# Gates and gated unit merged into the mixers' schedule, and the group norm's squares summed before the column sums, in a hybrid encoder layer on one Trainium2 core

## The chip, the core and the metric

The kernel runs on one core of a Trainium2 chip. A core has five engines with an instruction queue each: TensorE (PE: matmuls, with PEld its weight loads), VectorE (DVE), ScalarE (ACT), GpSimd (POOL) and SyncE (SP), which issues most of the DMAs. The on-chip memory is SBUF; matmuls write to PSUM. The metric is the time of one launch on the device in microseconds (us), as a median of several executions.

## The reference

One layer of a streaming encoder over 1024 tokens of width 1024, float32. The parts that the change touches:

```python
y = rms_norm(x)                        # norm 1
y @ w_in  ->  xa, gate (512 each: recurrence), u (512: state space)
# RG-LRU group
xc = causal_conv4(xa) + conv_b
r, i = sigmoid(xc @ wa + ba), sigmoid(xc @ wx + bx)      # by heads
a = exp(-8 * r * softplus(-lam))
h_t = a_t * h_{t-1} + sqrt(1 - a_t^2) * (i_t * xc_t)
A = h * gelu(gate)
# S5 group: diagonal complex state space in 32 groups of 16 channels
B = gelu(ssm(u) + d_skip * u)
B = B * sigmoid(B @ glu_w + glu_b)                       # gated unit
x = x + concat[rms_norm_A(A), rms_norm_B(B)] @ w_out
x = x + peer(rms_norm(x))              # product-key experts
out = rms_norm(x)
```

`peer` scores each token against two sets of 128 keys for 8 heads, takes 16 of the 256 best pairs and adds those experts' outputs.

## The kernel before, in words

`front()` does everything up to the output projection and takes about the first 430 us; `peer()` takes the rest. Activations are held transposed: features on the 128 partitions, tokens along the free dimension, ordered so that eight strided sets s of 128 tokens lie one behind the other. An fp32 product is made of three matmuls: each factor is split into a rounded part and a rest (names with h and l: `xh`, `xl`), and h*l, l*h and h*h are summed in PSUM. ACT makes the rounded part, DVE the rest. All compute instructions are recorded through one helper, so their profile lines all say L146, and the tile names tell them apart.

The mixers of `front()`:
- `us_first` and `us_second` project the two halves of the state-space input into the tiles `Vt[0]` and `Vt[1]` (PSUM tile `usp`).
- `quarter(q)`, four times, is the state-space group: it builds small operators (`WB`, `CAr`, `kp`), transposes `Vt` (`utp`), makes the inputs (`inr`, `ini`), rotates and scans them (`Wr`, `Zr`), makes the outputs (`yp`), applies gelu and stores into `yB`.
- `proj(grp)` makes 256 columns of the other projections in the PSUM tile `pj`: groups 0 and 1 the recurrence inputs `xa[0..3]`, groups 2 and 3 the gates. A group has 96 matmuls with 512 columns; the weights are loaded and split ahead in `wr`, `wh`, `wl`.
- `lru(m)`, four times, is the recurrence of 128 channels: convolution (`xc`), two gates (`gt`, sigmoid), tanh, exp, sqrt and a scan, which leaves its result in `xa[m]`.

Then follow `gates` and `last` (gelu of each `gate`, and `yA = xa * gate`), `glu` (splits `wg` and `yB`, makes `glp` with 96 matmuls, sigmoid `sg`, product into `yB`), `norm(0)` and `norm(1)` (split `yA` into `ah`, `al` and the new `yB` into `gh`, `gl`, square into `sq`, and sum over channels in `gs`), and `w_out(0)`, `w_out(1)`: 192 matmuls `wop` each, of which twelve make one half of a token block; their result times the group's `rg` is added to `h`. In `w_out(1)` the squares of the new `h` are summed (`jk`, `ss`) for norm 2. `peer()` starts with norm 2: `g2` is loaded, `xn = h * r2 * g2` is made for the blocks 5 to 7, transposed (`x2t`), split (`xGh`, `xGl`) and multiplied with the query weights (`wqr`, split into `wqh`, `wql`; result `qp`).

The order on each engine is fixed when the program is built. The class `Merge` holds a modelled time for each engine and runs Python generators as threads: the thread with the least time plus bias goes next, until its next `yield`; a `yield` of a name waits until another thread has set that flag. `mg.run` runs a list of (bias, thread) to its end. Engines then work in the order so recorded, and semaphores keep the data dependences. Before, there are three such runs one behind the other: mixers (state space 0.0, projections 1.0, recurrences 3.0), then gates and `last`, then gated unit, norms and output projection together.

SBUF is given out in two stacks, left and right, of pools that are closed in reverse order; a tile in the place of an older one waits until that one's last reader is done. ACT also issues some DMAs, in order with its own work: the eight loads of `h` and that of `g2` among them.

Of the kernel before, what the change touches and what calls it, by code (L numbers as in the profile page):

```python
# [18 lines left out]
P = 128  # L19
# [130 lines left out]
def front(tc, a, cst, nd, mg):  # L150
# [28 lines left out]

    pset = pools.open("fset")  # L180
# [76 lines left out]
    def us_first():  # L257

        w, held = [], [(pu if s < 2 else pj if s < 4 else pt)("usp")[:, :256] for s in range(L)]
        ws = wgroup(1024, 256, w, w0)  # L260
        for k in range(8):
            split_x(k)
            next(ws)
            yield
            for s in range(L):
                us_product(held[s], s, k, w)
            yield
        mg.flag("x")
        yield "rc"
        Vt[0] = p5.tile([P, 16, L, 16], F32, name="Vt", tag="Vt", bufs=2)  # L270
        for s in reversed(range(L)):
            us_out(0, s, held[s])
            yield
        mg.flag("us0")

    def us_second():
        w = []
        yield from wgroup(1280, 256, w)
        Vt[1] = p5.tile([P, 16, L, 16], F32, name="Vt", tag="Vt", bufs=2)
# [153 lines left out]
    def quarter(q):  # L433
# [71 lines left out]
        for h in range(2):  # L505
# [5 lines left out]
            S.activation(UT[:, 4 * h:4 * h + 4], q3(pp), AF.Copy)  # L511
        pq = [pt("inr"), pt("ini")]
# [164 lines left out]
    def s5_thread():  # L677
        yield "set"
        for q in range(4):
            yield from quarter(q)  # L680

    def proj_thread():
        yield from us_second()
        for grp in range(2):
            yield from proj(grp, [x[:, 3:] for x in xa[2 * grp:2 * grp + 2]], False)

    def lru_thread(ms):
# [3 lines left out]
        mg.flag("lru")  # L691

    lr_ = lru_thread(range(4))
    mg.run([(0.0, s5_thread()), (1.0, proj_thread()), (3.0, lr_)])
    pools.close("f5", "fset")
    pya = pools.open("fya")
    yA = [pya.tile([P, T], F32, name=f"yA{m}") for m in range(4)]
    pgate = pools.open("fgate")
    gate = [pgate.tile([P, T], F32, name=f"gate{m}") for m in range(4)]
    def gates():  # L700
        for grp in range(2):
            yield from proj(2 + grp, gate[2 * grp:2 * grp + 2], True)

    def last():
        for m in range(4):
            if m % 2 == 0:
                yield f"proj{2 + m // 2}"
            S.activation(gate[m], gate[m], AF.Gelu_apprx_tanh)
            sc = lambda x: x.rearrange("p (s c) -> p s c", c=P)
            V.tensor_tensor(sc(yA[m]), xa[m][:, 3:].rearrange("p (c s) -> p s c", s=L), sc(gate[m]), ALU.mult)  # L710
            yield

    mg.run([(0.0, gates()), (0.0, last())])
    pools.close("fl", "fw", "fin", "fxa")
    pools.close("fgate")


# [3 lines left out]
    ah = pg.tile([P, 4, T], F32R, name="ah")  # L721
    al = pg.tile([P, 4, T], F32R, name="al")
    po = pools.open("fo")
# [3 lines left out]
    wo = [{}, {}]  # L727

    def glu():
        for k in range(4):  # L730
            wg = pgw.tile([P, 512], F32, name="wg", tag="wg", bufs=2)
# [7 lines left out]
        for h in range(2):  # L739
            sl = slice(512 * h, 512 * h + 512)  # L740
            for ct in range(4):
# [7 lines left out]
                sg = pgw.tile([P, 512], F32, name="sg", tag="sg", bufs=2)  # L749
# [3 lines left out]
        mg.flag("glu")  # L753

# [16 lines left out]
    def norm(grp, ys, dh, dl):  # L771

        gs = pu("gs")
        for k in range(4):
# [5 lines left out]
            sq = po.tile([P, T], F32, name="sq2", tag="sq2")  # L780
            S.activation(sq, ys[k], AF.Square)
            yield
            for s in range(L):
                PE.matmul(gs[:, 4 * s + k:4 * s + k + 1], sq[:, s * P:(s + 1) * P], ones, start=True, stop=True)
            yield
        V.tensor_reduce(rg[grp], gs[:, :4 * L].rearrange("p (s k) -> p s k", k=4), AX.X, ALU.add)
        rsqrt_cols(mg, rv, rg[grp], rg[grp], 1.0 / 512)
# [37 lines left out]
    def group_b():  # L825
        yield from glu()
        yield from norm(1, [yB[:, k] for k in range(4)], gh, gl)
        yield from w_out(1)

    mg.run([(0.0, group_b()), (0.5, norm(0, yA, ah, al)), (1.0, group_a())])  # L830
    pools.close("fgw")
    pools.close("fo", "fg", "fya", "fkeep", "fps")
# [790 lines left out]
```

## Time and profile before

| what | us |
|---|---|
| median of 3 executions | 2782.96 (2782.08 to 2785.82) |
| the profiled execution | 2788.28 |
| its span, first to last instruction | 2786.5 |
| mean granted clock of TensorE, share of full | 0.957 |

| stretch of the span | what runs |
|---|---|
| 0 to 58 | loads, squares of `x`, first half of the state-space input, set-up |
| 58 to 291 | mixers, gates, the last product into `yA` |
| 291 to 430 | gated unit, group norms, output projection |
| 430 to 441 | norm 2 of the first blocks, first query weights |
| 441 to 2786 | PEER |

Times of rows are counted from the first instruction of the profiled execution. The span is 1.8 us shorter than that execution's time, and that execution is 5.3 us above the median, so differences are read inside the span and put onto the median. A row's idle time in brackets, with the sign <-, is the time in which the engine stood before it, and what ended it. ACTq and SPq are the DMA issues of these engines. Busy shares of PE come from modelled ends, so that a busy PE may still work slower than it could; the granted clock says how fast.

### The profile page before, as it was taken

What the parts mean: (1) busy time and instruction counts of PE and PEld (TensorE: products, weight loads), DVE (VectorE), ACT (ScalarE), POOL (GpSimd) and SP (SyncE); (2) the same over time, 40 slices, a digit from 0 to 9 for tenths busy, and PEclk for the clock granted to TensorE, in tenths of its full rate; (3) what the DMA queues carried; (4) which work ended last, traced back from release to release, by engine and by line L of the source; (5) the groups of instructions that cost most, each with busy time, mean ns of one, the idle gap of its engine ahead of it and who ended that gap; (6) DMA issues with size and microseconds to landing.
All of it is one profiled execution on the core that took longest, in us unless ns stands there. A gap on an engine that the chain in (4) does not pass through costs nothing.

```text
span 2786.5 us, 40983 instructions
## 1 busy us (share of the span) xinstructions
PE 2561.9 (92%) x14719; PEld 2314.2 (83%) x14719; DVE 2359.6 (85%) x4536; ACT 1322.1 (47%) x2401; POOL 1153.7 (41%) x777
## 2 busy tenths in 40 slices
PE   5888899888899999989989889999989999999997
PEld 5765688887799899989989878888878888888885
DVE  7787435499998999989989869999888889899996
ACT  5356424222286494773955753333433444333332
POOL 0000000023375474864745634455545555445550
PEclk9898899999999999999999989999999999999998
DMA  5110315366699899998998999999989999999994
GB/s 166 26 30 25 121 61 164 121 231 191 221 342 397 291 378 364 311 382 287 392 371 273 393 338 333 328 330 324 332 303 324 332 331 331 329 332 329 326 338 137
DMA packets 302140, 761.84 MB, mean 273 GB/s; under 512 B 28784, under 2 KB 126384, under 8 KB 296816
## 3 DMA queue, kind: packets, MB, share of 16 engines
q0 software_dynamic: 110592, 402.70, 40.4%
q1 hardware_dynamic: 184464, 345.19, 35.2%
q10 hardware_dynamic: 6880, 11.33, 1.2%
q8 instruction: 116, 1.90, 0.3%
q14 instruction: 88, 0.72, 0.1%
HBM read 668.81 MB, written 89.13 MB: 272 GB/s over the span
## 4 chain that ended last, share of the span: by engine, by line
PE 58%; DVE 23%; DMA 8%; ACT 6%; issue 5%; SPq 0%; ACTq 0%; DVEq 0%
PE vp L146 23%; PE ap L146 14%; PE total L146 6%; PE qp L146 4%; DVE row L146 3%; ACT ohB L146 3%; PE wop L146 3%; DVE hb L146 3%; DMA A_d<-aa 2%; DVE ix L146 2%; DVE ul L146 2%; PE gp L146 2%; DVE oh L146 2%; DMA ur<-in_uT_dram 2%; DVE v L146 2%
## 5 line engine op out<-in xcount | busy, mean ns | idle before, releaser
L1138 POOL DMA_INDIRECT row<-in_peer_u_dram,idx x384 | 569.2, 1482 | 1047.2 <-PE qp L146 541.2
L1138 POOL DMA_INDIRECT row<-in_peer_v_dram,idx x384 | 581.8, 1515 | 484.0 <-DVE hb L146 366.7
L146 PE MATMUL ap<-xDl,uh 128*128 128x320 f32 x2048 | 656.1, 320 | 19.5 <-ACT aa L146 19.2
L146 PE MATMUL ap<-xDh,ul 128*128 128x320 f32 x2048 | 650.9, 318 | 17.1 <-DVE ul L146 16.9
L146 PE MATMUL ap<-xDh,uh 128*128 128x320 f32 x2048 | 647.3, 316 | 0.0
L146 DVE SCALAR_TENSOR_TENSOR hb<-row,act,hb 128x1024 f32<-128x1024 f32 x384 | 492.0, 1281 | 7.3 <-DMA hb<-H_d 3.1
L146 DVE CUSTOM_DVE_ANT_0 row<-row,xg 128x1024 f32<-128x1024 f32 x384 | 458.3, 1217 | 6.0 <-DMA xg<-X_d 5.0
L146 PE MATMUL vp<-vl,hh 128*128 128x512 f32 x1024 | 400.2, 391 | 13.9 <-DVE h L146 11.6
L146 PEld LDWEIGHTS ap<-xDl,uh 128*128 128x128 f32 x2048 | 392.7, 192 | 22.9 <-ACT aa L146 20.9
L146 PEld LDWEIGHTS ap<-xDh,ul 128*128 128x128 f32 x2048 | 393.0, 192 | 22.1 <-DVE ul L146 20.7
L146 PE MATMUL vp<-vh,hl 128*128 128x512 f32 x1024 | 400.0, 391 | 0.0
L146 PE MATMUL vp<-vh,hh 128*128 128x512 f32 x1024 | 400.0, 391 | 0.0
L146 PEld LDWEIGHTS ap<-xDh,uh 128*128 128x128 f32 x2048 | 392.3, 192 | 0.0
L146 ACT ACTIVATE gq<-gt 128x640 f32<-128x640 f32 x128 | 175.1, 1368 | 337.9 <-DVE hr L146 325.8
L146 PE MATMUL gp<-ohB,ohA 128*128 128x128 f32 x1280 | 211.6, 285 | 44.1 <-ACT gs L146 23.6
L146 DVE TENSOR_TENSOR ul<-ur,uh 128x1024 fp32r<-128x1024 f32 x128 | 156.1, 1220 | 108.8 <-ACT uh L146 106.4
L146 PEld LDWEIGHTS vp<-vl,hh 128*128 128x128 f32 x1024 | 193.0, 188 | 55.2 <-DVE h L146 12.9
L146 PEld LDWEIGHTS gp<-ohB,ohA 128*128 128x128 f32 x1280 | 187.9, 195 | 53.4 <-ACT gs L146 25.5
L146 PEld LDWEIGHTS vp<-vh,hh 128*128 128x128 f32 x1024 | 192.9, 188 | 40.3
L146 PEld LDWEIGHTS vp<-vh,hl 128*128 128x128 f32 x1024 | 192.9, 188 | 39.4
L146 ACT ACTIVATE aa<-ap 128x320 f32<-128x320 f32 x194 | 85.1, 439 | 261.7 <-PE ap L146 237.7
L146 ACT ACTIVATE ohB<-ohB,kt 128x128 f32<-128x128 f32 x480 | 204.5, 503 | 0.0
(422 smaller groups left out, 4548.7 us busy)
## 6 DMA issues: line engine op xcount, KB each, us to landing
ur<-in_uT_dram SPq DMA_DIRECT2D x128, 512.0 KB
vr<-in_peer_v_dram SPq DMA_DIRECT2D x128, 512.0 KB
gt<-G_d SPq DMA_DIRECT2D x32, 1280.0 KB
G_d<-gs SPq DMA_DIRECT2D x19, 2048.0 KB
A_d<-aa SPq DMA_DIRECT2D x96, 320.0 KB
hr<-A_d SPq DMA_DIRECT2D x96, 320.0 KB
wqr<-in_wq_dram SPq DMA_DIRECT2D x32, 512.0 KB
S_d<-sc SPq DMA_DIRECT2D x64, 128.0 KB
```

The lines of the kernel that those rows point to most:

```text
L146: return fn(*args, **kw)
L1138: G.indirect_dma_start(out=r, out_offset=None, in_=a["peer_v" if at >= P else "peer_u"], in_offset=bass.IndirectOffsetOnAxis(ap=idx[n][:, ...
```

## The change

Five things change. First, the tiles `Vt` get a pool of their own, and `proj_thread` runs projection group 0, then `us_second`, then group 1, then the two gate groups, whose results go into the buffers of `Vt` once these have been transposed. Second, `last` becomes a thread beside the mixers and applies gelu in place. Third, `glu` (with the second norm and projection behind it) starts when the state-space thread has ended, while recurrences and gates still run; it may not go beyond the gated unit before the flags `wide` and `norm0`. Fourth, `norm` adds the squares of the four channel tiles on DVE into `rstdb` and then makes 8 column sums instead of 32, without the reduction; the second norm follows the first. Fifth, the pools of `ah`, `al` and of the output projection's weights are opened later and lie elsewhere.

```diff
--- before.py
+++ after.py
@@ -177,6 +177,7 @@
     S.dma_start(g1, a["g1"])
     S.dma_start(cols, a["cols"])
 
+    pvt = pools.open("fvt")
     pset = pools.open("fset")
 
     def t(shape, name):
@@ -267,7 +268,7 @@
             yield
         mg.flag("x")
         yield "rc"
-        Vt[0] = p5.tile([P, 16, L, 16], F32, name="Vt", tag="Vt", bufs=2)
+        Vt[0] = pvt.tile([P, 16, L, 16], F32, name="Vt", tag="Vt", bufs=2)
         for s in reversed(range(L)):
             us_out(0, s, held[s])
             yield
@@ -276,7 +277,7 @@
     def us_second():
         w = []
         yield from wgroup(1280, 256, w)
-        Vt[1] = p5.tile([P, 16, L, 16], F32, name="Vt", tag="Vt", bufs=2)
+        Vt[1] = pvt.tile([P, 16, L, 16], F32, name="Vt", tag="Vt", bufs=2)
         for s in range(0, L, 2):
             pp = pu("usp")
             for e in range(2):
@@ -509,6 +510,7 @@
                              Vt[q // 2][:, 8 * (q % 2) + 4 * h + j].rearrange("p s i -> p (s i)"), ident)
             yield
             S.activation(UT[:, 4 * h:4 * h + 4], q3(pp), AF.Copy)
+        mg.flag(f"ut{q}")
         pq = [pt("inr"), pt("ini")]
         for j in range(4):
             for o, w in zip(pq, win):
@@ -678,57 +680,50 @@
         yield "set"
         for q in range(4):
             yield from quarter(q)
+        mg.flag("s5")
 
     def proj_thread():
-        yield from us_second()
         for grp in range(2):
             yield from proj(grp, [x[:, 3:] for x in xa[2 * grp:2 * grp + 2]], False)
+            if grp == 0:
+                yield from us_second()
+        for grp in range(2):
+            yield f"ut{2 * grp + 1}"
+            y = pvt.tile([P, 2, T], F32, name="yA", tag="Vt", bufs=2)
+            yA.extend([y[:, 0], y[:, 1]])
+            yield from proj(2 + grp, yA[2 * grp:], True)
 
     def lru_thread(ms):
         for m in ms:
             yield f"proj{m // 2}"
             yield from lru(m)
-        mg.flag("lru")
-
-    lr_ = lru_thread(range(4))
-    mg.run([(0.0, s5_thread()), (1.0, proj_thread()), (3.0, lr_)])
-    pools.close("f5", "fset")
-    pya = pools.open("fya")
-    yA = [pya.tile([P, T], F32, name=f"yA{m}") for m in range(4)]
-    pgate = pools.open("fgate")
-    gate = [pgate.tile([P, T], F32, name=f"gate{m}") for m in range(4)]
-    def gates():
-        for grp in range(2):
-            yield from proj(2 + grp, gate[2 * grp:2 * grp + 2], True)
+            mg.flag(f"lru{m}")
+
+    yA = []
 
     def last():
         for m in range(4):
-            if m % 2 == 0:
-                yield f"proj{2 + m // 2}"
-            S.activation(gate[m], gate[m], AF.Gelu_apprx_tanh)
+            yield f"proj{2 + m // 2}"
+            S.activation(yA[m], yA[m], AF.Gelu_apprx_tanh)
+            yield f"lru{m}"
             sc = lambda x: x.rearrange("p (s c) -> p s c", c=P)
-            V.tensor_tensor(sc(yA[m]), xa[m][:, 3:].rearrange("p (c s) -> p s c", s=L), sc(gate[m]), ALU.mult)
-            yield
-
-    mg.run([(0.0, gates()), (0.0, last())])
-    pools.close("fl", "fw", "fin", "fxa")
-    pools.close("fgate")
-
-
+            V.tensor_tensor(sc(yA[m]), xa[m][:, 3:].rearrange("p (c s) -> p s c", s=L), sc(yA[m]), ALU.mult)
+            yield
+
+        mg.flag("mixed")
+
+    mg.run([(0.0, s5_thread()), (0.5, proj_thread()), (0.0, lru_thread(range(4))), (3.0, last())], until="s5")
+    pools.close("f5", "fset")
     pg = pools.open("fg")
     gh = pg.tile([P, 4, T], F32R, name="gh")
     gl = pg.tile([P, 4, T], F32R, name="gl")
-    ah = pg.tile([P, 4, T], F32R, name="ah")
-    al = pg.tile([P, 4, T], F32R, name="al")
-    po = pools.open("fo")
     pgw = pools.open("fgw")
     wgh = pgw.tile([P, 4, 512], F32R, name="wgh")
     wgl = pgw.tile([P, 4, 512], F32R, name="wgl")
-    wo = [{}, {}]
 
     def glu():
         for k in range(4):
-            wg = pgw.tile([P, 512], F32, name="wg", tag="wg", bufs=2)
+            wg = pgw.tile([P, 512], F32, name="wg", tag="g", bufs=2)
             nc.sync.dma_start(wg, a["glu_w"][k * P:(k + 1) * P, :])
             S.activation(wgh[:, k], wg, AF.Copy)
             V.tensor_tensor(wgl[:, k], wg, wgh[:, k].bitcast(F32), ALU.subtract)
@@ -746,11 +741,27 @@
                     PE.matmul(pp, wgl[:, k, cs], gh[:, k, sl], start=False, stop=False)
                     PE.matmul(pp, wgh[:, k, cs], gh[:, k, sl], start=False, stop=(k == 3))
                 yield
-                sg = pgw.tile([P, 512], F32, name="sg", tag="sg", bufs=2)
+                sg = pgw.tile([P, 512], F32, name="sg", tag="g", bufs=2)
                 S.activation(sg, pp, AF.Sigmoid, bias=cols[:, ct, 9:10])
                 V.tensor_tensor(yB[:, ct, sl], yB[:, ct, sl], sg, ALU.mult)
                 yield
         mg.flag("glu")
+
+    def group_b():
+        yield from glu()
+        yield "wide"
+        yield "norm0"
+        yield from norm(1, [yB[:, k] for k in range(4)], gh, gl)
+        yield from w_out(1)
+
+    mg.add([(4.0, group_b())])
+    mg.run([], until="mixed")
+    pools.close("fl", "fw", "fin", "fxa")
+    pa_ = pools.open("fa")
+    ah = pa_.tile([P, 4, T], F32R, name="ah")
+    al = pa_.tile([P, 4, T], F32R, name="al")
+    po = pools.open("fo")
+    wo = [{}, {}]
 
     rg = [keep.tile([P, L], F32, name=f"rg{g}") for g in range(2)]
 
@@ -770,21 +781,23 @@
 
     def norm(grp, ys, dh, dl):
 
-        gs = pu("gs")
+        gs, tot = pu("gs"), rstdb
         for k in range(4):
             g_ = cols[:, k, 7 + grp:8 + grp]
             S.activation(dh[:, k], ys[k], AF.Copy, scale=g_)
             yield
             V.scalar_tensor_tensor(dl[:, k], ys[k], g_, dh[:, k].bitcast(F32), ALU.mult, ALU.subtract)
             yield
-            sq = po.tile([P, T], F32, name="sq2", tag="sq2")
+            sq = po.tile([P, T], F32, name="sq2", tag="sq2") if k else tot
             S.activation(sq, ys[k], AF.Square)
             yield
-            for s in range(L):
-                PE.matmul(gs[:, 4 * s + k:4 * s + k + 1], sq[:, s * P:(s + 1) * P], ones, start=True, stop=True)
-            yield
-        V.tensor_reduce(rg[grp], gs[:, :4 * L].rearrange("p (s k) -> p s k", k=4), AX.X, ALU.add)
-        rsqrt_cols(mg, rv, rg[grp], rg[grp], 1.0 / 512)
+            if k:
+                V.tensor_tensor(tot, tot, sq, ALU.add)
+                yield
+        for s in range(L):
+            PE.matmul(gs[:, s:s + 1], tot[:, s * P:(s + 1) * P], ones, start=True, stop=True)
+        yield
+        rsqrt_cols(mg, rv, rg[grp], gs[:, :L], 1.0 / 512)
         mg.flag(f"norm{grp}")
         yield
 
@@ -822,14 +835,9 @@
         yield from w_out(0)
         yield from wo_half(1)
 
-    def group_b():
-        yield from glu()
-        yield from norm(1, [yB[:, k] for k in range(4)], gh, gl)
-        yield from w_out(1)
-
-    mg.run([(0.0, group_b()), (0.5, norm(0, yA, ah, al)), (1.0, group_a())])
-    pools.close("fgw")
-    pools.close("fo", "fg", "fya", "fkeep", "fps")
+    mg.flag("wide")
+    mg.run([(0.5, norm(0, yA, ah, al)), (1.0, group_a())])
+    pools.close("fo", "fa", "fgw", "fg", "fvt", "fkeep", "fps")
     return pools, h, ss
 
 
```

The rows of the two programs at three places follow. TensorE in the first quarter of the state-space group, where `kp` makes the operators, `utp` the transposed inputs and `inr`, `ini` the inputs of the scan; first before, then after:

```order
L146 MATMUL kp_674<-CAr,Br 16x128
L146 MATMUL kp_674<-CAn,Bi 16x128
L146 MATMUL utp<-ident,Vt 128x128 x8
L146 MATMUL usp<-wl,xh 128x256
L146 MATMUL usp<-wh,xl 128x256
L146 MATMUL usp<-wh,xh 128x256
...
L146 MATMUL inr<-UT,win 64x128 x2
L146 MATMUL ini<-UT,win 64x128 x2
```

```order
L146 MATMUL kp_683<-CAr,Br 16x128
L146 MATMUL kp_683<-CAn,Bi 16x128
L146 MATMUL pj<-xl,wh 128x512
L146 MATMUL pj<-xh,wl 128x512
L146 MATMUL pj<-xh,wh 128x512
...
L146 MATMUL utp<-ident,Vt 128x128 x4
...
L146 MATMUL utp<-ident,Vt 128x128 x4
L146 MATMUL inr<-UT,win 64x128 x2
```

Before, 12 small matmuls of `us_second` stood between `utp` and `inr`. Now 24 `pj` stand ahead of the first four `utp` and 12 more ahead of the other four, 36 in all before `inr`. At the other end of the mixers, the last `pj` was followed by 2 `wop` and the first of 96 `glp`; now 41 `glp` stand ahead of the last `pj`, and 43 more behind it ahead of the first `wop`.

VectorE around the last product into `yA` (of the fourth recurrence, `xa_77`) and the first norm's sums, before and after:

```order
L146 TENSOR_TENSOR yA_2024<-xa_77,gate_2031 128x1024
L146 TENSOR_TENSOR wgl<-wg,wgh 128x512
L146 SCALAR_TENSOR_TENSOR al<-yA_2021,cols,ah 128x1024
L146 TENSOR_TENSOR wol<-wor,woh 128x512
L146 TENSOR_TENSOR gl<-yB,gh 128x1024
...
L146 TENSOR_REDUCE rg_2364<-gs 128x8
L146 TENSOR_TENSOR yB<-yB,sg 128x512
L146 TENSOR_SCALAR sq_84<-rg_2364 128x8
```

```order
L146 TENSOR_TENSOR yA<-xa_77,yA 128x1024
L146 TENSOR_TENSOR yB<-yB,sg 128x512
L146 SCALAR_TENSOR_TENSOR al<-yA,cols,ah 128x1024
L146 TENSOR_TENSOR wol<-wor,woh 128x512 x2
...
L146 TENSOR_TENSOR rstdb<-rstdb,sq_2550 128x1024
L146 TENSOR_TENSOR yB<-yB,sg 128x512
L146 TENSOR_SCALAR sq_84<-gs 128x8
L146 TENSOR_TENSOR yB<-yB,sg 128x512
L146 SCALAR_TENSOR_TENSOR gl<-yB,cols,gh 128x1024
```

The four `wgl` and the four `gl` of the gated unit, and three of its eight products `yB`, now stand ahead of this place; three additions into `rstdb` (per norm) have come in.

ScalarE at the seam to `peer()`, where `g` is the load of `g2` and `jk` the squares of the finished `h` (the names in brackets are the semaphores waited for), before and after:

```order
L146 ACTIVATE sq_2758<-yB 128x1024 [waits PE_49]
L886 DMA g_3253<-in_g_dram 128x1024 [waits Activation_49]
L146 ACTIVATE sq_2784<-yB 128x1024 [waits PE_49,Activation_49]
...
L146 ACTIVATE jk,ss<-h_2378 128x1024 [waits DVE_49,Activation_49]
L146 ACTIVATE r_3256<-vv 128x3 [waits DVE_49]
L146 ACTIVATE jk,ss<-h_2377 128x1024 [waits DVE_49,Activation_49]
```

```order
L146 ACTIVATE jk,ss<-h_2453 128x1024 [waits DVE_49,Activation_49]
L146 ACTIVATE jk,ss<-h_2452 128x1024 [waits DVE_49,Activation_49]
L146 ACTIVATE jk,ss<-h_2451 128x1024 [waits DVE_49,Activation_49]
L894 DMA g_3201<-in_g_dram 128x1024 [waits PE_49,Activation_49]
L146 ACTIVATE r_3204<-vv 128x3 [waits DVE_49]
```

The load of `g2` stood among the squares of the second norm and now stands behind the last of the eight `jk`, whose space it takes over; with it the `r2` and `xn` of the first blocks move behind the end of the output projection. ACT has 38 table loads ahead of `peer()` where it had 32.

## The prediction

> **What bounds the kernel now.** The change touches the first 440 us alone; behind them every engine keeps its rows. I read the busy time per stretch first. The columns are start:end, length, then busy us (instructions) of TensorE (PE), its weight loads, VectorE (DVE), ScalarE (ACT) and GpSimd, then granted clock, DMA share and GB/s.
>
> ```profile
> 58.00:193.00 135.00, 122.85 (x850) 101.05 (x849) 108.58 (x191) 56.00 (x93) 0.00 (x0) 0.90 0.14 32
> 193.00:291.00 98.00, 74.89 (x302) 52.27 (x302) 67.45 (x75) 52.07 (x65) 0.00 (x0) 0.84 0.10 31
> 291.00:430.00 139.00, 129.58 (x608) 107.90 (x608) 61.35 (x94) 50.89 (x69) 0.00 (x0) 0.94 0.23 85
> 66.50:193.00 126.50, 114.59 (x762) 93.74 (x758) 102.42 (x168) 49.10 (x81) 0.00 (x0) 0.91 0.13 30
> ```
>
> The mixers (58 to 291) keep neither PE nor DVE full; 291 to 430 is a PE stage. The chain of waits shows what lies between them:
>
> ```profile
> 275.93 11.20 PE pj L146 x48
> 287.12 11.46 issue
> ...
> 390.42 39.08 PE wop L146 x171
> ```
>
> PE stops at the last `pj`, stands 11.46 us, then pays one 512-wide matmul per 39.08/171 = 0.2285 us to the end of the output projection. The standing costs more, since the clock falls with it:
>
> ```profile
> 292.00:294.00 2.00, 0.00 (x0) 0.00 (x0) 0.00 (x0) 0.00 (x0) 0.00 (x0) 0.55 1.02 405
> ...
> 308.00:310.00 2.00, 2.00 (x8) 1.57 (x7) 1.61 (x2) 2.00 (x4) 0.00 (x0) 0.69 0.37 130
> ```
>
> So from 298.6 (287.12 + 11.46) to about 309 PE works at half rate. The timeline gives the marks I count from (rows picked out):
>
> ```profile
> 66.49 0.68 DVE L146 TENSOR_TENSOR Wr<-inr,Ec 128x508 f32<-128x508 f32 x1
> 287.87 6.97 ACTq L796 DMA_DIRECT2D h<-in_x_dram  x7
> 288.95 1.99 DVE L146 TENSOR_TENSOR yA<-xa,gate 128x1024 f32<-128x1024 f32 x1 [1.12 <-ACT gate L146]
> 295.42 1.13 ACT L146 ACTIVATE ah<-yA,cols 128x1024 fp32r<-128x1024 f32 x1
> 325.94 0.19 DVE L146 TENSOR_REDUCE rg<-gs 128x8 f32<-128x32 f32 x1 [5.67 <-PE gs L146]
> 331.07 1.41 DVE L146 SCALAR_TENSOR_TENSOR h<-wop,rg,h 128x512 f32<-128x512 f32 x2
> 429.09 0.39 PE L146 MATMUL wop<-woh,gh 128*128 128x512 f32 x1
> 431.33 0.18 ACT L146 ACTIVATION_READ_ACCUMULATOR jk<-h 128x1 f32 x1
> 440.68 0.69 PE L146 MATMUL qp<-xGh,wql 128*128 128x384 f32 x1
> ```
>
> Three marks follow: T, the end of the last `yA` product, 291; E, the end of the last `wop`, 429.5; Q, the first `qp` of the unbroken run, 440.7. So E - T is 138.5 and Q - E is 11.2.
>
> **Term 1, the mixers (T).** The waits of DVE from 66 to 291, by what ended them (us in total, times, longest):
>
> ```profile
> DVE CAr L146 <- PE yp L146: 8.3, 2, 5.4
> DVE Wr L146 <- PE inr L146: 7.8, 3, 3.5
> DVE gate L146 <- PE pj L146: 7.5, 3, 4.7
> DVE tau L146 <- ACT tau L146: 6.2, 2, 6.0
> DVE pr__1113 L146 <- PE wtp L146: 2.6, 1, 2.6
> ```
>
> DVE is busy 102.42 + 67.45 = 169.9 of the 224.5 us from 66.5. Work that now stands ahead of the last product is among these groups, from which terms 2 and 3 draw too (count, busy us, mean ns; rows picked out):
>
> ```profile
> L146 DVE TENSOR_TENSOR gl<-yB,gh 128x1024 fp32r<-128x1024 f32 x4 | 4.9, 1221 | 0.4 <-ACT gh L146 0.4
> L146 DVE TENSOR_TENSOR wgl<-wg,wgh 128x512 fp32r<-128x512 f32 x4 | 2.7, 687 | 4.8 <-ACT wgh L146 4.8
> L146 DVE TENSOR_TENSOR yB<-yB,sg 128x512 f32<-128x512 f32 x8 | 5.5, 688 | 5.2 <-ACT sg L146 5.1
> L146 PE MATMUL gs<-ones,sq 128*128 128x1 f32 x128 | 16.3, 257 | 0.0
> L146 DVE SCALAR_TENSOR_TENSOR xn<-h,r,g 128x1024 f32<-128x1024 f32 x5 | 6.3, 1280 | 1.2 <-PE x2t L146 1.2
> L146 ACT ACTIVATE sq<-yA 128x1024 f32<-128x1024 f32 x4 | 4.2, 1051 | 2.5 <-PE gs L146 2.5
> L146 ACT ACTIVATE woh<-wor 128x512 fp32r<-128x512 f32 x16 | 9.8, 623 | 22.3 <-PE wop L146 13.8 <-DMA wor<-in_w_out_dram 8.4
> L146 ACT ACTIVATE sg<-glp,cols 128x512 f32<-128x512 f32 x8 | 5.4, 685 | 12.5 <-PE glp L146 7.2 <-DVE sq L146 5.2
> ```
>
> The four `gl`, the four `wgl` and three `yB` products make 4.9 + 2.7 + 3 x 0.69 = 9.7, so 179.5 in all. The start moves: 36 `pj` stand ahead of `inr` in the first quarter, 36 x 0.2285 = 8.2 us, less some 1.5 that run before the transposes' input is ready (an estimate): the first `Wr` comes at 73 instead of 66.5. What is open is DVE's pace. Before, it was (108.58 + 67.45)/233 = 0.755 over the stage, 102.42/126.5 = 0.81 in its first part and 67.45/98 = 0.69 in the tail. In the new order recurrence rows stand where DVE waited for `yp`, `wtp` and `inr` (8.3 + 2.6 + 7.8), because the first two inputs are ready sooner; and the tail no longer consists of one recurrence and gates that wait on PE (7.5). Against that stand six more table loads on ACT. I take 0.85, bounded by 0.755 (nothing filled) and 0.90: T = 73 + 179.5/0.85 = 284, from 311 down to 272. PE allows it: 122.85 + 74.89 = 197.7 busy, plus 43 `glp` that now stand between the last `pj` and the first `wop` (9.8), is 207.5 of 226, a share of 0.92 against 0.91 from 66.5 to 193. Term 1 is a gain of **7**.
>
> **Term 2, T to E.** `ah` can't start at T: the `h` loads are ACT's DMA issues and wait until `xa`'s space is free, so the queue holds `ah` back (4.4 us in the trace: 291 to 295.42). About five of the eight issues still stand behind that wait now, so T + 3. ACT then does four `ah`, four squares and, between them, five `woh` and three `sg`: 4 x 1.13 + 4 x 1.05 + 5 x 0.62 + 3 x 0.69 = 13.9, so its fourth square ends at T + 17; the last addition into `rstdb` (1.2) and eight `gs` put the sums at T + 20; the chain from sums to the first `h` took 331.07 - 325.94 = 5.1 and has a `gl` and two `wol` between, so T + 26. The two banks of `wop`, twelve matmuls each, let 24 of the 384 be done by then. The other 360 cost 360 x 0.2285 = 82; 8 `gs` 1; at the half boundary I keep 3.5 of stall. E - T is 26 + 82 + 4.5 = 113, a gain of **25.5**. It is the 21.8 us of `glp` (96 x 0.2285) that now lie under the mixers' tail and the wait, and the idle and half-rate time after 287. Of the 128 `gs` (16.3 us of PE) 112 go, some 14 us, which is in the figure too; they put six additions of 1.22 (as `gl`) on DVE, which has 61.35 busy of 139 here: hidden, except the last before each sum, counted above. Bounds: the first `h` at T + 21 (no queueing on ACT) or T + 33 (as slow as 331.07 - 298.57 after the start), so 108 to 120.
>
> *The clock.* From the last `pj` (T - 4, as 287.1 is to 291) to the first `h`, PE has 55 `glp`, 24 `wop` and 8 `gs`, 79 x 0.2285 + 1 = 19 us for 30, so it stands 11 in pieces; the longest, before the first `h`, is about 4.5 (T + 20 and six `wop` to T + 26). In the trace an 11.46 us stand cost half rate for some 10.6 us, 5.3 lost; if the shorter one does the same, the sum loses 5. [...]
>
> **Term 3, E to Q.** ACT's rows, shown with the change, hold the price: `g2` is loaded only behind the eighth `jk`. Before, it was loaded during the first half:
>
> ```profile
> issues: line engine op xcount, KB each, median us to landing
> g<-in_g_dram ACTq DMA_DIRECT2D x1, 512.0 KB
> 351.17 0.34 ACTq L886 DMA_DIRECT2D g<-in_g_dram  x1
> GB/s 0 0 0 0 0 0 0 0 0 0 0 0 0 0 191 82 109 246 328 382 382 355 355 300 219 137 164 137 55 55 0 0 0 0 0 0 0 0 0 0
> ```
>
> The row of GB/s is 350 to 356 in fortieths, so the bytes end at 354.5, 3.3 after issue. `jk` ends E + 2.0; `g2` lands E + 5.4; three blocks then need 3 x (1.28 + 2 x 0.69) = 8.0 of DVE (`xn`, and two subtractions of a `wgl`'s size), and transposing and splitting the last 1.3: Q = E + 14.7. Before, two blocks' `xn` were done early and the chain went through a weight load, whose first buffers now come free sooner:
>
> ```profile
> 431.54 6.75 DMA wqr<-in_wq_dram
> ```
>
> Loss **3.5**, bounded by 2 and 10 (a load of `g2` as slow as that of `wqr`, and a queueing of 3 ahead of it).
>
> **The sum.** 7 + 25.5 - 3.5 = 29. Everything behind Q is kept. The profiled execution took 2788.28 around its span of 2786.5; the median is 2782.96, so 2783 - 29 = **2754** for a median.
>
> **Rivals.** In all of them time after = 2783 - (313 - T), with terms 2 and 3 kept.
> (a) *The pace rises to 0.90*: for it, 26 us of the waits above name PE, and PE's filling brings its clock from 0.84 in the tail to 1.0. Against: the recurrences' own ACT steps (6.2 for `tau`) stay. T = 272.5, 2742.
> (b) *Waits only change names*: DVE keeps 0.755 because PE, at a share of 0.91 already, hands it `inr` and `yp` no sooner. T = 311, 2781, no change.
> (c) *Slower: ACT's in-order queue.* Sigmoid, tanh, exp, sqrt, gelu and sin of three threads now interleave, with 38 table loads for 32. Each sits in a queue behind which `UT`, `Yt`, `gt` and `wh` stand, and DVE and PE wait for those: 6 x 1.28 = 7.7 us, and each may delay both engines. It decides once DVE's pace falls under 179.5/240 = 0.748; at 0.72, T is 322 and the time 2792. For it: the largest single DVE wait here, 6.0, is for ACT's `tau`. Against: ACT is busy 108 of 233 us. A load costs what it lasts, and the next instruction follows at once:
>
> ```profile
> 249.42 1.28 ACT L146 ACT_TABLE_LOAD   x1
> 250.71 1.06 ACT L146 ACTIVATE gate<-gate 128x1024 f32<-128x1024 f32 x1
> ```
>
> [...] The trace has the load at 1.28 and a gap of 0.01 behind it.
>
> **How the numbers follow.** Forecast 0.65, (a) 0.17, (b) 0.10, (c) 0.08. The forecast's own range is T from 279 to 293 with term 2 from 108 to 120 and the clock's 5: 2744 to 2770. Reaching into (a) and toward (b) gives **2736 to 2776**. This kernel can be told from no change at about 0.2%, 5.6 us: faster than 2777.4 takes the forecast, (a) and a fifth of (b), 0.84; (b)'s remainder and the edges 0.08; slower 0.08.
>
> **What would show it.** Right: last `yA` product near 284; DVE's share from 73 to there near 0.85 and PE's clock over 0.9; `glp` running where PE stood idle; the first `h` update about T + 26; last `wop` near 397; `g2` issued behind the last `jk`, `qp` steady near 412; then equal times to the end. Wrong: T beyond 300, waits on ACT's tables among DVE's largest, a second half-rate stretch longer than 5 us before the first `h`, or a seam over 20 us.

## The result, and the profile after

The changed kernel takes 2762.85 us (median of 5, 2759.9 to 2771.57) where the kernel before took 2785.77 (5 runs, 2782.08 to 2791.45): a ratio of 0.9927, 95% interval 0.9908 to 0.9947. That is 23 us less; the forecast was 29 less and 2754, inside a range of 2736 to 2776. The profiled execution took 2759.9, the fastest of the five, with a span of 2758.1. One execution of a later run ("gates after" below) took 4165.8 us at a granted clock of 0.556 and is left out of its ratio. The reading below is of the marks inside the span.

| mark | before | predicted | after |
|---|---|---|---|
| first `Wr` | 66.5 | 73 | 73.2 |
| T, last product into `yA` ends | 291 | 284 | 279.3 |
| first update of `h` | 331.1 | T + 26 | 307.5 (T + 28.2) |
| E, last `wop` ends | 429.5 | 397 | 397.6 |
| Q, `qp` runs unbroken | 440.7 | 412 | 416.1 |
| from Q to the first `ap` of PEER | 261.9 | kept | 261.9 |

The busy time per stretch, of the kernel after (columns as in the prediction):

```profile
73.20:193.00 119.80, 101.25 (x693) 79.73 (x690) 109.62 (x166) 58.99 (x87) 0.00 (x0) 0.96 0.11 28
193.00:279.30 86.30, 81.44 (x412) 61.04 (x412) 65.65 (x84) 58.61 (x73) 0.00 (x0) 1.00 0.17 51
73.20:279.30 206.10, 182.69 (x1104) 140.77 (x1101) 175.26 (x250) 117.61 (x160) 0.00 (x0) 0.98 0.14 38
279.30:397.60 118.30, 107.53 (x450) 86.09 (x448) 57.51 (x82) 42.61 (x58) 0.00 (x0) 0.91 0.28 100
```

In the mixers VectorE is busy 175.26 of 206.1 us, a pace of 0.850. TensorE's clock is 1.00 in the mixers' tail, where it was 0.84. The timeline of the kernel after, rows picked out (the third is the table load ahead of the last gelu):

```profile
73.22 0.69 DVE L146 TENSOR_TENSOR Wr<-inr,Ec 128x508 f32<-128x508 f32 x1 [4.15 <-PE inr L146]
...
256.67 2.31 DVE L146 TENSOR_TENSOR_SCAN xa<-r__2104,tau 128x1024 f32<-128x1024 f32 x1
...
274.78 1.28 ACT L146 ACT_TABLE_LOAD   x1 [3.84 <-PE pj L146]
...
277.17 2.12 DVE L146 TENSOR_TENSOR yA<-xa,yA 128x1024 f32<-128x1024 f32 x1 [2.09 <-ACT yA L146]
...
290.83 0.50 PE L146 MATMUL wop<-wol,ah 128*128 128x512 f32 x1 [2.50 <-DVE wol L146]
...
307.52 1.59 DVE L146 SCALAR_TENSOR_TENSOR h<-wop,rg,h 128x512 f32<-128x512 f32 x2
...
356.11 0.50 PE L146 MATMUL wop<-wol,gh 128*128 128x512 f32 x1 [2.99 <-DVE wol L146]
...
405.04 1.28 DVE L146 SCALAR_TENSOR_TENSOR xn<-h,r,g 128x1024 f32<-128x1024 f32 x1 [3.12 <-DMA g<-in_g_dram]
...
411.65 1.28 DVE L146 SCALAR_TENSOR_TENSOR xn<-h,r,g 128x1024 f32<-128x1024 f32 x1 [1.79 <-DMA X_d<-xn]
...
416.11 0.69 PE L146 MATMUL qp<-xGl,wqh 128*128 128x384 f32 x1 [0.56 <-DVE xGl L146]
```

The chain of waits of the kernel after names what stands between these marks:

```profile
284.74 4.66 DMA wor<-in_w_out_dram
...
299.53 3.22 PE gs L146 x16
...
344.45 1.68 PE gs L146 x16
...
349.03 4.03 DMA ur<-in_uT_dram
353.14 1.06 ACT uh L146
...
356.11 41.45 PE wop L146 x174
...
399.61 5.41 DMA g<-in_g_dram
405.04 1.30 DVE xn L146
406.36 5.20 DMA X_d<-xn
```

Three things in it were not in the forecast. A load of output weights takes 4.66 us at 284.74, and ScalarE's splits behind it wait. At the half boundary a load of `ur` and the split `uh`, work of PEER, stand on ScalarE ahead of two `woh`. The chain runs through them from 349.0 to 356.1, but TensorE has `wop` to do for most of that time and stands 2.99 us ahead of 356.1. At the seam the third `xn` waits for the store of the first into `X_d`, since there are two buffers. The waits of VectorE from 66 to 300 have changed, too:

```profile
DVE Wr L146 <- PE inr L146: 13.3, 3, 7.8
DVE yA L146 <- ACT yA L146: 3.8, 2, 2.1
DVE xa L146 <- PE pj L146: 3.7, 3, 2.0
```

Those for `yp`, `tau` and `wtp` are gone or small, those for `inr` have grown from 7.8 to 13.3.

### The profile page after: what moved, and what is told of

Same layout as the page of the kernel before. It is cut to its first block, busy times and chain, and to the rows that moved or that the text cites. A ratio compares the mean times of both kernels' runs of the same rounds, so it can differ in the third digit from the quotient of the medians.

```text
span 2758.1 us, 40787 instructions
## 1 busy us (share of the span) xinstructions
PE 2538.0 (92%) x14623; PEld 2289.4 (83%) x14623; DVE 2364.1 (86%) x4540; ACT 1329.9 (48%) x2407; POOL 1164.7 (42%) x777
## 4 chain that ended last, share of the span: by engine, by line
PE 57%; DVE 25%; DMA 9%; issue 5%; ACT 3%; POOL 1%; SPq 0%; ACTq 0%; DVEq 0%; POOLq 0%
PE vp L146 24%; PE ap L146 15%; PE total L146 6%; DVE row L146 5%; PE wop L146 3%; PE qp L146 3%; DMA A_d<-aa 3%; PE gp L146 2%; DVE ix L146 2%; DVE oh L146 2%; DVE ul L146 2%; DMA ur<-in_uT_dram 2%; DVE v L146 2%; PE pj L146 1%; DVE hb L146 1%
## 5 line engine op out<-in xcount | busy, mean ns | idle before, releaser
L1146 POOL DMA_INDIRECT row<-in_peer_u_dram,idx x384 | 581.6, 1515 | 1014.4 <-DVE ix L146 521.6
L146 PE MATMUL ap<-xDl,uh 128*128 128x320 f32 x2048 | 654.8, 320 | 16.3 <-ACT aa L146 16.1
L146 PEld LDWEIGHTS ap<-xDh,ul 128*128 128x128 f32 x2048 | 392.2, 192 | 25.5 <-DVE ul L146 24.1
```

Source lines behind the costliest of these rows:

```text
L146: return fn(*args, **kw)
L1146: G.indirect_dma_start(out=r, out_offset=None, in_=a["peer_v" if at >= P else "peer_u"], in_offset=bass.IndirectOffsetOnAxis(ap=idx[n][:, ...
```

## The experiments

Each run was timed in five rounds beside the kernel before, on four chips in all; the ratio is to before on the same chip. Since a few us are near what the times can tell, I read the marks of each profile as well. All marks are in us from the first instruction; differences in the text are taken before rounding and can differ from those of the table by 0.1.

| kernel | last scan ends | last `pj` ends | T | E | Q | ratio to before, 95% |
|---|---|---|---|---|---|---|
| before | 274.0 | 287.1 | 290.9 | 429.5 | 440.7 | 1 |
| changed | 259.0 | 274.4 | 279.3 | 397.6 | 416.1 | 0.9927 (0.9908 to 0.9947) |
| second input half first | 290.5 | 277.3 | 292.5 | 407.1 | 425.6 | 0.9939 (0.9916 to 0.9962) |
| 32 column sums | | | 280.6 | 404.9 | 421.4 | 0.9929 (0.9903 to 0.9956) |
| gated unit after | 259.0 | 268.1 | 272.0 | 401.2 | 417.9 | 0.9910 (0.9878 to 0.9943) |
| swap alone | 263.0 | 283.1 | 286.9 | 425.2 | 436.1 | 0.9988 (0.9972 to 1.0004) |
| gates after | 262.0 | 298.0 | 303.0 | 423.8 | 440.4 | 1.0020 (1.0007 to 1.0034) |
| gates alone | 286.0 | 276.0 | 288.1 | 426.5 | 443.3 | 1.0021 (1.0003 to 1.0039) |
| weights below splits | | | 279.7 | 395.6 | 405.1 | 0.9865 (0.9839 to 0.9890) |
| and `h` loaded later | | | 280.3 | 391.5 | 400.7 | 0.9871 (0.9847 to 0.9894) |
| and four buffers | | | 282.1 | 389.7 | 398.9 | 0.9850 (0.9828 to 0.9871) |
| and TensorE kept busy | | | 280.6 | 387.8 | 397.1 | 0.9860 (0.9846 to 0.9874) |

**Undoing the swap.**

```diff
 def proj_thread():
+    yield from us_second()
     for grp in range(2):
         yield from proj(grp, ...)
-        if grp == 0:
-            yield from us_second()
```

> Undoes one part: the second half of the state-space input is projected ahead of the first two recurrence inputs again, all else as in the changed kernel. Theory: the first rotation (Wr) comes 6 to 7 us earlier (near 66.5 in place of 73.2), but the recurrences' rows are no longer there to fill VectorE's waits, and its pace falls from 0.85 to about 0.80, so that the last product into yA ends at 66.5 + 175/0.80 = 285 in place of 279.3: the median is 3 to 9 us above the changed kernel's. Rival: the swap only moves the start; the pace stays 0.85, the last product ends near 272.5, and the median is about 6 us below the changed kernel's.

T was 292.5 and not 285, E 9.5 later than in the changed kernel; the median of 2772.1 is 0.9939 of before. At the marks the rival is out. The rotation's start hardly moved (71.4), so the first half of the theory fails as well: VectorE waits 5.0 for `inr` there too. VectorE's busy share from 71.4 to T was 0.80 (176.66/221.07), as expected, but the reason is in the table: the fourth recurrence's scan ended at 290.5 instead of 259.0. The recurrences begin later: the last `pj` of group 0 ended at 139.2 and the first scan at 176.7, where the changed kernel has 93.8 and 134.7. The timeline of this run:

```profile
288.19 2.29 DVE L146 TENSOR_TENSOR_SCAN xa<-r__2270,tau 128x1024 f32<-128x1024 f32 x1
290.51 2.00 DVE L146 TENSOR_TENSOR yA<-xa,yA 128x1024 f32<-128x1024 f32 x1
```

The gates were ready long before (last `pj` at 277.3); the recurrence came last.

**32 column sums again.**

```diff
-    sq = po.tile(...) if k else tot
+    sq = po.tile(...)
...
-    if k:
-        V.tensor_tensor(tot, tot, sq, ALU.add)
-for s in range(L):
-    PE.matmul(gs[:, s:s + 1], tot[:, s * P:(s + 1) * P], ones, ...)
+    for s in range(L):
+        PE.matmul(gs[:, 4 * s + k:4 * s + k + 1], sq[:, s * P:(s + 1) * P], ones, ...)
+V.tensor_reduce(rg[grp], gs..., AX.X, ALU.add)
```

> Undoes one part: each norm makes 32 column sums on TensorE and a reduction again, without the additions into rstdb; all else as in the changed kernel. Theory: the first norm's sums fall into the stand before the first h and cost little there, the second norm's 24 further sums (some 5 us) lie on TensorE's full path: from the last product into yA to the last wop 122 to 128 us in place of 118.3, the median 4 to 9 us above the changed kernel's. Rival: the sums were hidden anyway and the additions cost as much as they save: within 2 us of the changed kernel.

From T to E it took 124.3 (404.9 - 280.6) where the changed kernel took 118.3: 6 us, the theory's lower half. Q was 5.3 later. The ratio, 0.9929, doesn't tell it from the changed kernel's 0.9927, so this part is worth 5 to 7 us at the marks and nothing that the times resolve.

**The gated unit held back.**

```diff
 def glu():
+    V.tensor_copy(gh[:, :, 0], yA[3][:, 0:4])
+    V.tensor_copy(wgh[:, :, 0], yA[3][:, 0:4])
     for k in range(4):
...
-mg.add([(4.0, group_b())])
...
-mg.run([(0.5, norm(0, yA, ah, al)), (1.0, group_a())])
+mg.run([(0.0, group_b()), (0.5, norm(0, yA, ah, al)), (1.0, group_a())])
```

> Undoes one part: the gated unit's splits of yB and of its weights wait for the last product into yA (two 128x4 copies of that product's first values into the tiles, overwritten afterwards, make them wait), so that all 96 glp follow the mixers as before; the gates stay beside the mixers. Theory: the last product comes 5 to 11 us earlier (the 9.7 us of VectorE work at its pace), the way from there to the last wop grows by the 21.8 us of glp less what fills stands, 12 to 20 us; the median is 4 to 12 us above the changed kernel's. Rival: the gated unit's early start only exchanges one place for another, and the gates beside the mixers bring all: within 2 us of the changed kernel.

T came 7.3 earlier, as the theory had it; but E came only 3.6 later and Q 1.8 later, and the ratio of 0.9910 is not above the changed kernel's. The rival holds for the time, though not in saying that the gates bring all (see the gates alone). The 96 `glp` do go back behind T, and the stretch from T to E grows from 118.3 to 129.2; but it grows by 11 and not by 21.8, since 72 of them run ahead of the first `h`, where TensorE would wait anyway (306.5 here, 307.5 in the changed kernel; from there to E it is 94.7 in place of 90.0), and the mixers give back 7.3. From the chain of this run:

```profile
277.99 6.71 DMA wor<-in_w_out_dram
...
288.13 5.00 PE glp L146 x14
```

Behind T both orders wait for the same thing first, a load of output weights whose place comes free there.

**The swap alone**, in the kernel before:

```diff
-    yield from us_second()
     for grp in range(2):
         yield from proj(grp, ...)
+        if grp == 0:
+            yield from us_second()
-mg.run([(0.0, s5_thread()), (1.0, proj_thread()), (3.0, lr_)])
+mg.run([(0.0, s5_thread()), (0.5, proj_thread()), (0.0, lr_)])
```

> The kernel before with one part of the change alone: the first two recurrence inputs are projected ahead of the second half of the state-space input, with the changed kernel's biases for the three mixer threads (0.0, 0.5, 0.0); gates, gated unit, norms and placement stay as before. Theory (from the run without the swap, whose last product into yA ended at 292.7, later than before): the swap is what shortens the mixers; the last product ends 8 to 15 us earlier than before's 291, the way from there to the last wop stays 136 to 141 us, and the median is 7 to 14 us under before's. Rival: the swap pays only with the gates beside the mixers; the last product ends at 287 to 293 and the median is within 4 us of before's.

It fell between: T 4.0 earlier, E 4.3 earlier, the median 4 us under before's and the interval of the ratio reaching 1. The theory's 8 to 15 is out. The scan ended 11 us earlier (263.0 for 274.0), but now the gates came last, as the timeline shows:

```profile
260.69 2.28 DVE L146 TENSOR_TENSOR_SCAN xa<-r__1988,tau 128x1024 f32<-128x1024 f32 x1
...
284.94 1.99 DVE L146 TENSOR_TENSOR yA<-xa,gate 128x1024 f32<-128x1024 f32 x1 [1.12 <-ACT gate L146]
```

**The gates held back**, in the changed kernel:

```diff
 for grp in range(2):
     yield f"ut{2 * grp + 1}"
+    yield "lru3"
     y = pvt.tile(...)
+    V.tensor_copy(y[:, :, 0], xa[3][:, 3:5])
+    V.tensor_copy(y[:, :, 512], xa[3][:, 3:5])
```

> Undoes one part of the changed kernel: the gates' projections wait for the fourth recurrence's scan (two copies of its result into the gates' tiles, overwritten afterwards, make them wait); the gated unit still starts when the state-space thread ends and now fills TensorE while the recurrences finish. Theory: the gates beside the recurrences are the larger part of the shortened mixers; with 144 of their 192 pj (33 us) behind the last scan, the last product into yA ends 4 to 12 us later than 279.4 and the last wop 3 to 8 us later than 397.6, the median 3 to 8 us above the changed kernel's. Rival: TensorE is full in the mixers in either order, so that the order of pj and glp is indifferent: last wop within 2 us of 397.6.

T was 23.7 later and E 26 later, far over both. The scan ended at 262.0, as in the changed kernel, and then TensorE still had 144 of the gates' 192 `pj` before it (timeline):

```profile
259.67 2.29 DVE L146 TENSOR_TENSOR_SCAN xa<-r__2003,tau 128x1024 f32<-128x1024 f32 x1 [0.26 <-ACT r__2003 L146]
...
300.84 2.12 DVE L146 TENSOR_TENSOR yA<-xa,yA 128x1024 f32<-128x1024 f32 x1 [2.09 <-ACT yA L146]
```

This wait is stricter than the order before, whose first gate product stood at 252.3, so the 26 us are an upper bound on what the change gained here.

**The gates alone**: the edits of the first three runs together, of which the first lines are:

```diff
+    yield from us_second()
...
+V.tensor_reduce(rg[grp], gs..., AX.X, ALU.add)
...
+    V.tensor_copy(gh[:, :, 0], yA[3][:, 0:4])
```

> The changed kernel with three parts undone at once: the second half of the state-space input first again, 32 column sums in each norm, and the gated unit held back until the last product into yA; what is left is the gates beside the recurrences (and the changed placement). Theory (the swap and the gates pay only together: the swap alone moved the last wop by 4.3 us, undoing it in the changed kernel by 9.5): the gates alone end the mixers at 281 to 288, 3 to 10 us ahead of before's 291, the last wop lies at 418 to 426 where before's was at 429.5, and the median is 0 to 8 us under before's. Rival: the gates bring their whole gain by themselves, as holding them back cost 26 us at the last wop: last product by 276, last wop by 415, median 14 us or more under before's.

The theory holds at T and E: T 288.1, E 426.6, and the recurrence last (scan to 286.0, `pj` to 276.0). For the time it was too good: Q lies 2.6 behind before's, since the seam of the changed placement stays, and the ratio is 1.0021.

**The placement.**

```diff
-pa_ = pools.open("fa")
-ah, al = ...
 po = pools.open("fo")
+pa_ = pools.open("fa")
+ah, al = ...
```

> One line of the placement is changed: the pool of the output projection's weights and squares is opened ahead of the pool of ah and al, so that ah and al (free after the first half of the projection) lie where norm 2 places its tiles. Theory: g2 is loaded during the second half, the first two blocks' xn are made there, and the two loads of ur no longer stand among the split weights at the half boundary: from the last wop to the first steady qp 9 to 11.5 us in place of 18.5, the stop at the half boundary 2 to 3.5 in place of 5 to 7; the median 8 to 13 us below the changed kernel's. Rival: the seam is held by the query weights' load whatever g2 does: 15 us or more from the last wop to qp, and within 4 us of the changed kernel.

From E to Q it took 9.4 where the changed kernel took 18.5, and the ratio went from 0.9927 to 0.9865. The rival is out: no wait for `g2` is left at the seam, and with `xn` of two blocks made early the third finds its buffer free. The chain of this run around the half boundary:

```profile
350.68 3.32 DMA wor<-in_w_out_dram
...
357.25 38.40 PE wop L146 x168
```

Its timeline has TensorE's stand there:

```profile
355.43 0.50 PE L146 MATMUL wop<-wol,gh 128*128 128x512 f32 x1 [2.12 <-DVE wol L146]
```

The other half of the expectation rested on a misreading: the 5 to 7 us at the half boundary of the changed kernel were the length of the chain there, and TensorE's stand was 2.99. `uh` is gone from it here, and the stand is 2.12, now behind a load of `wor`: E came 1.9 earlier and no more.

**The loads of `h` behind the first weights**, on top of it:

```diff
-for b in reversed(range(L)):
-    S.dma_start(h[b], xv[:, b])
...
 def wo_half(half):
...
+    if half == 0:
+        for b in reversed(range(L)):
+            nc.sync.dma_start(h[b], xv[:, b])
```

> On top of the kernel with the weights below the splits: the eight loads of h (512 KB each) are issued by SyncE behind the first loads of output weights instead of by ScalarE ahead of them. Theory: after the last product into yA the transfers run at about 410 GB/s for 10 us with loads of h that nothing needs yet, ScalarE's queue is held by their issues and the second pair of output weights lands 4.7 us after its issue; without this, ah starts within 1 us of the last product in place of 2.5, and the first h update comes 3 to 6 us earlier than 27 us after it; last wop 3 to 6 us earlier than 395.7, median 3 to 6 us under the kernel it builds on. Rival: ScalarE's own work (four ah, four squares, the weights' and the gated unit's instructions, 14 us) sets the first h; it moves by less than 2 us.

The first `h` came at T + 22.8 (303.1) and not T + 27.0, E 4.2 earlier. The theory holds at the marks. The times don't show it: 2747.62 and a ratio of 0.9871, on another chip, beside 0.9865.

**Four buffers for the weights as loaded**, on top of it:

```diff
-r = po.tile([P, 512], F32, name="wor", tag="wor", bufs=2)
+r = po.tile([P, 512], F32, name="wor", tag="wor", bufs=4)
```

> As the run with the later loads of h, and four buffers in place of two for the output weights as loaded (4 KB more). [...] Rival: the waits for wol only become waits for the norm's sums, which come last whatever the weights do: last wop moves by less than 3 us beyond the run with the later loads of h.

The first `h` is at T + 20.5, E 5.9 ahead of the run with the weights below the splits, but only 1.7 ahead of the run before it, inside the rival's 3, and the waits for `wol` (10.0 in the changed kernel) are 0.2. The clock fell to 0.50 here, too, from 298.84 on. TensorE's longest wait is now the one for the first `h`. The half rate begins 0.02 us into that wait (298.82), after 2.64 us of work in the 2.8 before it, and outlasts it by 5.8 us (to 309.1), so the wait did not bring it on (waits of TensorE from 270 to 312, the row of the timeline, then windows):

```profile
PE wop L146 <- DVE h L146: 4.5, 1, 4.5
```

```profile
303.32 0.80 PE L146 MATMUL wop<-wol,ah 128*128 128x512 f32 x1 [4.50 <-DVE h L146]
```

```profile
296.00:298.80 2.80, 2.64 (x19) 2.09 (x18) 1.43 (x2) 0.33 (x1) 0.00 (x0) 1.00 1.06 408
298.84:300.00 1.16, 0.00 (x0) 0.00 (x0) 1.14 (x3) 1.12 (x2) 0.00 (x0) 0.50 0.43 152
300.00:302.00 2.00, 0.00 (x0) 0.00 (x0) 1.28 (x4) 1.97 (x3) 0.00 (x0) 0.50 0.03 7
306.00:308.00 2.00, 2.00 (x6) 1.56 (x5) 2.00 (x2) 2.00 (x3) 0.00 (x0) 0.50 0.00 0
```

At 2744.77 (2737.25 to 2747.28) and 0.9850 of before, this is the fastest of the kernels here by median, beyond the changed kernel's interval.

**TensorE kept busy** in that wait:

```diff
+if grp == 0:
+    dm = pu("dm")
+    for i in range(16):
+        PE.matmul(dm, wgh[:, 0, :P], wgh[:, 1], start=True, stop=True)
```

> On top of the run with later loads of h and four buffers: sixteen matmuls of 512 columns on the gated unit's weights, whose result nothing reads, stand behind the first norm's column sums on TensorE, to fill its stand of 4.5 us before the first h update. They are added work that the reference doesn't need. Theory: the stand is what halves the clock from 299 to 309; filled, the granted clock stays at 1.0 there, the 5.7 us of wop that ran at half rate take 2.8 less, and the last wop comes 2 to 3.5 us earlier against the first h update (which was 87.3 us ahead of the last wop's update), the median 1 to 4 us under the run it builds on. Rival: the first wop behind the first h wait for VectorE's updates and not for TensorE's clock: the clock stays up, but first h to last h stays within 1 us of 87.3.

From the first update of `h` to the end of the last `wop` it took 85.9 us (387.8 - 301.9) instead of 87.2: 1.3 gained, between the two; the median is the same (2744.81). The clock did not stay up, but fell ahead of the filling matmuls (`dm`) and came back sooner (windows of this run, then two rows of its timeline):

```profile
290.00:292.00 2.00, 1.70 (x9) 1.12 (x7) 2.00 (x4) 2.00 (x4) 0.00 (x0) 1.00 1.04 340
292.00:294.00 2.00, 0.77 (x2) 0.43 (x3) 2.00 (x3) 2.00 (x4) 0.00 (x0) 1.00 0.96 334
294.00:296.00 2.00, 1.84 (x10) 1.06 (x9) 1.97 (x3) 0.93 (x1) 0.00 (x0) 1.00 1.01 394
296.00:298.00 2.00, 2.00 (x13) 2.00 (x13) 0.00 (x0) 0.00 (x0) 0.00 (x0) 0.59 0.81 305
...
304.00:306.00 2.00, 2.00 (x10) 1.65 (x9) 2.00 (x2) 2.00 (x3) 0.00 (x0) 1.00 0.00 0
```

```profile
298.05 6.29 PE L146 MATMUL dm<-wgh 128*128 128x512 f32 x16
...
304.18 0.39 PE L146 MATMUL wop<-wol,ah 128*128 128x512 f32 x1
```

The filling itself ran at half rate for most of its 6.29 us, so that the first `wop` behind the first `h` came 2.3 us after it (304.2 - 301.9) instead of 0.8 (303.3 - 302.5). The half rate behind the first `h` fell from 6.6 us to 1.3, worth some 2.6 us (an estimate, half of the difference), and the later start took 1.5 of that back.

## Why the prediction was right, point by point

**Direction and range** were right, and the sum of 29 was near: at Q the changed kernel is 24.6 us ahead, at the end of the span 28.4, in the medians 22.9. Each term was off by 4 to 5 us: the first gained 4.6 more than forecast, the others 5.3 and 3.8 less, so that the errors cancelled in part. That is luck.

**Term 1** gained 11.6 where 7 was predicted. The start of the first rotation (73.2) and the pace (0.850) came as forecast; the part of the sum that was off is VectorE's work ahead of T, 175.3 instead of 179.5. The gated unit accounts for little of that: its four `wgl`, its four `gl` and two of the `yB` products, not three, lie ahead of T, 9.0 of the 9.7 counted. One product into `xa` and two `wl` (1.7) now lie ahead of the first `Wr`, and the rest is overlap of VectorE's rows: their durations add up to 16.3 us more than the busy time, and to 14.3 more before. The reasons given for the pace hold in part. VectorE's waits for `yp`, `wtp` and `tau` did go, that for `inr` grew to 13.3. And a pace of VectorE is not what sets T, so that 0.850 came out as picked is luck, too. Two chains meet in the last product: the fourth recurrence's scan and the last gate's `pj`. Before, the scan ended at 274.0 and the `pj` at 287.1. The swap alone brings the scan forward by 11 and leaves the `pj` last (283.1). The gates alone bring the `pj` to 276.0 and make the scan last (286.0). With both, 259.0 and 274.4. So neither part has more than a few us by itself (E 4.3 and 2.9 earlier), and undoing either in the changed kernel moves T by 13 or, with a wait stricter than the old order, by 24. The prediction had both ingredients, but as one number for a pace; it could not have said what one part is worth.

**Term 2** gained 20.2 (138.5 against 118.3) where 25.5 was predicted. The first `h` came at T + 28.2 and not T + 26, behind the load of `wor` of 4.66 us and with the `gs` at half rate (3.22 for what takes 1.68). From there to E it took 90.0 where the sum had 87: the second norm's `gs` took 1.7 and not 1, and 5.3 us of this stretch were at half rate (to 309.4, and from 357.2 to 360.6), worth some 2.6 (an estimate, half of them). The stand at the half boundary was 2.99, within the 3.5 that I kept. The sentence that the gain "is the 21.8 us of `glp`" was wrong: holding the gated unit back costs 3.6 at E and nothing that the times show. The column sums were worth 6, where "some 14" of busy time was named. That figure was miscounted: each sum is two records, so 32 of the 128 `gs` records stay and 96 go, 12 us at the mean of before, and of them only the second norm's lie on TensorE's path (with 32 sums the first `h` came at T + 28.3, as without).

The clock's loss was left out of the sum of 29, and it was not small. The half rate in the changed kernel lasted from 292.3 to 309.4, with TensorE standing in pieces; nearly all of it lies ahead of the first `h`:

```profile
292.40:307.50 15.10, 10.56 (x33) 8.28 (x32) 10.61 (x19) 10.63 (x15) 0.00 (x0) 0.50 0.26 80
```

The 10.56 us of work at half rate would take about half of that at the full one (an estimate from the granted 0.50), so that TensorE lost some 5 us there. That is as much as the 5 from the row of before. How much of it delays the first `h` no run shows, since TensorE also waited for split weights there. The clock fell at 292.3 with no stand above 2.50 us from 280 on, and in the run that kept TensorE busy at 296.4 with none above 1.23 from 282 on, where the stand of before was 11.46. Of the signs of being wrong that were named, the one on the clock came in this form: not a second half-rate stretch, but one of 15.2 us ahead of the first `h`.

**Term 3** lost 7.3 (18.5 against 11.2) where 3.5 was predicted, inside its bounds of 2 to 10. The mechanism was the one named; two prices were missing. `g2` took 5.41 us to land beside two loads of query weights of its size and one of 128 KB, instead of the 3.3 until its last bytes when alone, and the third `xn` waited for the store of the first, since the two that were early before now come one behind the other. Moving the weights' pool took the whole loss away.

**The rivals.** (a), the higher pace, had its condition come true, as the clock in the tail rose to 1.00, but not its pace: 0.850 and not 0.90, and T (279.3) lies between its 272.5 and the forecast's 284. (b) and (c) did not come: the 38 table loads are there, yet VectorE's waits on ScalarE in the mixers are small, the largest sum 3.8 us, for `yA`, and `tau` is no longer among the waits. One load does stand in the chain that ends the mixers, the one at 274.78: the last `yA` product waits 2.09 for its gelu where it waited 1.12 before, about 1 us of T. What stays open: the run with the gates after and that with the gates alone are slower than before by 0.2% in the times, though their profiles have Q at 440.4 and 443.3 beside before's 440.7. The stretch from the first `ap` of PEER to the end differs by several us between profiles (2074.7 to 2086.5) with no order to it that I could find, and a difference of that size can't be put to a part of the change.

## What to carry to other kernels

Where an end is the meeting of two chains, take down when each of them ends, and cost an edit by the later one: a part that shortens one chain is worth no more than the gap to the other, and two such parts can be worth much more together than the sum of each alone. Look where a changed order puts the pools, not only the instructions: what lies last and highest decides what the next stage can load early, and here one line of placement was worth as much as a good part of the change. Behind a point where much space comes free at once, sort the loads by when they are needed; here that brought 4.2 us at E, which the times do not tell apart.

## What the runs showed of the hardware that I had not expected

TensorE's clock fell to half while the engine was still busy for most of the time: in the run that kept it busy, 4.3 of the 6 us from 290 to 296, with no stand above 1.23 us, and it fell at 296.4, within the column sums (128x1). It came back after 6.8 us of work, and after 10.7 us in the kernel before. In the clock's records the stretches at half rate between 60.1 and 450 us last 3.4, 6.8, 10.2, 17.1 or 20.5 us in the kernel before (seven) and 3.4, 10.2, 17.1 or 20.5 us in the changed kernel (four); those ahead of the first `h` last 17.1 us in both, 292.2 to 309.3 and 292.3 to 309.4. A load of 512 KB took 3.3 us to its last bytes by itself, and 5.4 to land beside two others of its size and one of 128 KB.
